# Moving one recurrent unit, keeping a second copy of q, and re-pacing the sample work in a hybrid decoder step

## The chip, the cores and the metric

The kernel runs on one core of a Trainium2 chip. The metric is the device time of one execution in microseconds (us). A core has five engines that each run their own instructions in order: PE (TensorE, the matrix multiplier, with its weight loads shown apart as PEld), DVE (VectorE), ACT (ScalarE), POOL (GpSimd) and SP (SyncE). SP does no arithmetic here: it issues most of the DMA transfers, in order, and a transfer that has to wait holds up those behind it. PE writes into PSUM banks, the other engines move results from there to SBUF, and DMA moves data between SBUF and DRAM.

## What is computed

One inference step of one decoder layer, for a prompt of 2048 tokens and for 8 sample requests of 4 tokens each, in float32:

```
a = rmsnorm(h); [qa|fa|ia|ga|qb|kb|vb] = a @ w_in          # 1024 -> 7 x 512
h = h + concat(HGRN2(qa,fa,ia,ga), DilatedAttn(qb,kb,vb)) @ w_o
h = h + ConvFFN(rmsnorm(h))                                # 1024 -> 2816 -> 1024
h = h + sigmoid(rmsnorm(h) @ w_ple_gate) * (p @ w_ple_proj)
y = rmsnorm(h)
```

HGRN2 is a gated linear recurrence over the tokens, with 4 heads of width 128 and a 128x128 state per head. It is evaluated in chunks; its output is normalised, multiplied by the gate made from `ga`, and put into `mix`. DilatedAttn is softmax attention with 8 heads of width 64 over three dilations (the last 128 tokens, every 4th of 512, every 16th of 2048). The sample requests do the same with a carried state and a window of cached keys and values.

## The kernel before

**Stages.** Three stages follow each other: the projections (`in_phase`, called once per block of tokens: block 0 is tokens 0 to 1023, block 1 the rest and the 32 sample tokens), attention (`attn_phase`), and the trunk (output projection, ConvFFN, embedding gate). A product of float32 matrices is made of three matmuls on parts that were split in two.

**Projections.** `ORDERS` gives the order of the seven groups of a block. The groups with two letters (`qa fa ga`) are made with features on the partitions, in 12 tiles of 24 matmuls each (`feature_group`); the others (`i q k v`) with tokens on the partitions, one tile per 128 tokens (`token_group`). After each tile the generator yields, and the main program runs one or two steps of the recurrence (`pace` says how many). In block 1 the accumulators rotate over two PSUM buffers. In this stage a scheduler sets the order of each engine's instructions, from priorities.

**Recurrent units.** `hgrn_unit(u, heads)` handles 512 tokens for two of the four heads. There are eight units (0 to 7), each of 11 steps: loads; three level steps of many small matmuls with DVE work on their results; two steps that finish the local matrix and transpose the keys; two that update the state and make the output; normalisation; and, in the last step, transposes and the product with the gate `g`. Units 0 to 3 are done before the marker `"H"` in `ORDERS[1]`, which stands after `ga`; units 4 to 6 beside `q k v`. Unit 7 is done in the attention stage, in a variant called `apart` (more and smaller steps, one rsqrt done on POOL, its matmuls on two PSUM banks called `s1` and `s2`).

**Attention.** Four pairs of heads (p = 0 to 3) are worked through in blocks (p, di, c) of four residues each: c is a chunk of 512 queries; for di = 0 the queries of a block are one residue mod 4 of the chunk (`qs[:, hh, 512*c + r : 512*c + 512 : 4]`, every fourth value in memory), for di = 1 they are 128 neighbours. A block has 4 units (8 where its keys are over 256 wide), 40 units per pair. One turn of the main loop starts one unit: its scores (two matmuls per head, with q as the weights and the high and low part of the keys moving), a masked row minimum on DVE, the exponential on ACT, transposes on PE two or three units later and the product with the values some units after that. `stage` loads q and k of a chunk from DRAM into two stage tiles, and `stack` splits them into `qS`, `kH`, `kL` (rounding and subtracting on POOL, casting keys on ACT). `merge` combines the two dilations. The PE order of this stage is written out by hand; the other engines' order is the scheduler's.

**Side work in attention.** `others()` gives steps that are put between the turns: 33 steps of unit 7, then 43 of `attn_sample` (the sample requests' attention, of which 32 each load up to 1 MB of cached keys or values into one of four `skt` tiles and multiply with them), then 17 of `hgrn_sample`. One step is done per turn in the first 29 turns and every second turn from there.

**Memory.** Six stage tiles rotate: two from each of two pools, and the two tiles `ssq` and `rb` of the projections. The pools of the attention stage take the memory that the projections leave; before the change unit 7's pools stay open beside them until unit 7 is done.

## Time and profile before

| what | us |
|---|---|
| median of 3 runs | 2956.08 |
| lowest and highest run | 2954.88, 2963.84 |
| the profiled execution | 2961.47 |
| its span, first to last instruction | 2959.4 |
| PE busy | 2887.6 (98% of the span) |
| DVE / ACT / POOL busy | 2154.3 / 1317.7 / 692.0 |
| stretches of the span: block 1's projections with recurrent units | about 375 to 806 |
| attention (pairs p = 0, 1, 2, 3 start at) | 806 (807.7, 899.4, 986.8, 1082.3) |
| trunk | about 1170 to 2959 |

The profile has a page with sums over the whole execution, and views that answer for a stretch of time: busy times by window, single instructions in order of time, the waits of an engine and what ended them. Busy time of one instruction reaches from its start to the end of its result, so two pipelined matmuls overlap: what a matmul costs the engine is read from the distance of two starts. `PEclk` is the share of the full TensorE clock that was granted in a stretch. DMA share is the mean busy share of 16 DMA engines; it can read a little over 1.

### The profile page before, as it was taken

Reading aid. Unit: us, or ns where it says so; the run is one execution under the profiler, and the core shown is the slowest. Engines: PE = TensorE matmul, PEld = TensorE weight load, DVE = VectorE, ACT = ScalarE, POOL = GpSimd, SP = SyncE. Lnnn points to the kernel's source line nnn. Section 1 sums busy time; section 2 is a strip of 40 time slices with the busy share of each in tenths; the row PEclk is TensorE's granted clock in tenths of the full one; section 3 lists DMA queues with packets and bytes.
Section 4 is the critical chain, followed back from the end, with each engine's and each line's share of the span. In section 5 each row is a group of like instructions: output and inputs, shape, how many; then the busy total and the mean of one; then the engine's idle time right before and its main releaser. Section 6 shows DMA issues by size and latency. Waiting matters only on the chain. (4 is left out here: it accounts for less than half of the span.)

```text
span 2959.4 us, 52469 instructions
## 1 busy us (share of the span) xinstructions
PE 2887.6 (98%) x18895; PEld 2697.3 (91%) x18895; DVE 2154.3 (73%) x4684; ACT 1317.7 (45%) x2856; POOL 692.0 (23%) x842
## 2 busy tenths in 40 slices
PE   8999999999989999999999999999999999999998
PEld 8987789987776678999999999999999999999998
DVE  6656857747685567579987889776679777778787
ACT  5333423222376676335444444544444544444453
POOL 1343322212343463003334332000102000101001
PEclk9999999999999999999999999999999999999999
DMA  5898633334549986775765668777779777778784
GB/s 182 296 355 302 220 105 104 109 92 130 173 123 272 253 208 200 263 260 190 243 200 192 207 216 292 238 237 239 257 241 313 245 235 244 260 246 297 262 283 148
DMA packets 341171, 660.92 MB, mean 223 GB/s; under 512 B 62960, under 2 KB 136816, under 8 KB 339120
## 3 DMA queue, kind: packets, MB, share of 16 engines
q1 hardware_dynamic: 297760, 452.13, 48.1%
q0 software_dynamic: 36944, 136.89, 14.3%
q10 hardware_dynamic: 6208, 68.56, 6.4%
q8 instruction: 149, 2.44, 0.3%
q14 instruction: 110, 0.90, 0.1%
HBM read 509.46 MB, written 213.92 MB: 244 GB/s over the span
## 5 line engine op out<-in xcount | busy, mean ns | idle before, releaser
L154 PE MATMUL mm<-w 128*128 128x348 f32 (+3 forms) x3620 | 1160.6, 321 | 0.8 <-DVE w L1493 0.7
L155 PE MATMUL mm<-w 128*128 128x348 f32 (+3 forms) x3492 | 1111.8, 321 | 1.7 <-DVE w L192 1.6
L153 PE MATMUL mm<-w 128*128 128x348 f32 (+3 forms) x3492 | 1103.0, 322 | 10.1 <-ACT s L1289 5.9
L154 PEld LDWEIGHTS mm<-w 128*128 128x128 f32 x3620 | 680.7, 188 | 3.2 <-DVE w L1493 1.4
L153 PEld LDWEIGHTS mm<-w 128*128 128x128 f32 x3492 | 653.0, 188 | 18.2 <-ACT s L1289 8.6
L155 PEld LDWEIGHTS mm<-w 128*128 128x128 f32 x3492 | 655.4, 188 | 3.3 <-DVE w L192 2.6
L192 DVE TENSOR_TENSOR w<-raw,w 128x512 fp32r<-128x512 f32 x586 | 425.0, 731 | 177.5 <-ACT w L191 166.1
L191 ACT CAST w<-raw 128x512 fp32r<-128x512 f32 x586 | 360.8, 621 | 418.2 <-PE mm L155 290.8
L1331 POOL DMA_DIRECT2D w<-wd_d x231 | 123.7, 536 | 897.4 <-PE mm L155 791.4
L1347 DVE TENSOR_TENSOR h<-h,mm 128x348 f32<-128x348 f32 (+1 forms) x504 | 247.5, 507 | 44.3 <-PE mm L155 42.8
L840 ACT ACTIVATE P<-P,st 128x256 f32<-128x256 f32 (+3 forms) x256 | 134.1, 527 | 68.0 <-DVE st L839 66.1
L839 DVE CUSTOM_DVE_ANT_0 P<-S,mask 128x256 f32<-128x256 f32 (+3 forms) x256 | 105.0, 448 | 72.8 <-PE S L835 45.3
L1289 ACT COPY s<-mm 128x348 f32<-128x348 f32 (+1 forms) x198 | 87.9, 444 | 156.3 <-PE mm L155 156.3
L358 PE MATMUL mm<-wl,xh 128*128 128x512 f32 x352 | 140.4, 400 | 0.1
L357 PE MATMUL mm<-wh,xh 128*128 128x512 f32 x352 | 140.2, 401 | 0.0
L359 PE MATMUL mm<-wh,xl 128*128 128x512 f32 x352 | 139.8, 398 | 0.0
L153 PE MATMUL mm<-xh,wh 128*128 128x384 f32 (+2 forms) x384 | 124.6, 329 | 6.8 <-ACT xh L253 5.0
L155 PE MATMUL mm<-xh,wl 128*128 128x384 f32 (+2 forms) x384 | 124.3, 327 | 3.5 <-DVE wl L278 3.4
L154 PE MATMUL mm<-xl,wh 128*128 128x384 f32 (+2 forms) x384 | 124.1, 326 | 0.1
L192 DVE TENSOR_TENSOR dw<-draw,dw 128x512 fp32r<-128x512 f32 x77 | 74.3, 967 | 55.8 <-ACT dw L191 55.4
L278 DVE TENSOR_TENSOR wl<-wraw,wh 128x512 fp32r<-128x512 f32 x104 | 86.6, 852 | 33.7 <-POOL wh L159 28.9
L159 POOL TENSOR_SCALAR wh<-wraw 128x512 fp32r<-128x512 f32 x96 | 76.6, 811 | 135.9 <-PE mm L154 47.9
(369 smaller groups left out, 5087.3 us busy)
## 6 DMA issues: line engine op xcount, KB each, us to landing
w<-wd_d POOLq DMA_DIRECT2D x231, 512.0 KB, 5.4
wd_d<-dw SPq DMA_DIRECT2D x77, 512.0 KB
out_sk_dram<-in_cache_k_dram ACTq DMA_DIRECT2D x56, 584.0 KB
out_sv_dram<-in_cache_v_dram ACTq DMA_DIRECT2D x56, 584.0 KB
raw<-in_w_gate_dram SPq DMA_DIRECT2D x110, 256.0 KB
raw<-in_w_up_dram SPq DMA_DIRECT2D x110, 256.0 KB
wraw<-in_w_in_dram SPq DMA_DIRECT2D x104, 256.0 KB
raw<-w_gate_d SPq DMA_DIRECT2D x88, 256.0 KB
```

The source lines that it names most:

```text
L153: PE.matmul(ps, lhsT=wh, rhs=xh, start=first, stop=False, skip_group_check=read)
L154: PE.matmul(ps, lhsT=wh, rhs=xl, start=False, stop=False, skip_group_check=read)
L155: return PE.matmul(ps, lhsT=wl, rhs=xh, start=False, stop=last, skip_group_check=read)
L191: A.copy(w[:, 0], raw)
L192: V.tensor_sub(w[:, 1], raw, f32(w[:, 0]))
L357: PE.matmul(ps, lhsT=xh[k][:, js], rhs=wh, start=k == 0, stop=False)
L358: PE.matmul(ps, lhsT=xh[k][:, js], rhs=wl, start=False, stop=False)
L359: ins = PE.matmul(ps, lhsT=xl[k][:, js], rhs=wh, start=False, stop=k == NK - 1)
L839: V.tensor_tensor_reduce(pe, s[:, w * i:w * i + w], bl.mask, 1.0, 3e38, ALU.add, ALU.min, mn)
L840: recent[:] = [A.activation(pe, pe, AF.Exp, bias=mn, scale=-1.0, accum_out=st[:, bl.r, hh, 0:1])]
L1331: G.dma_start(t, wd_d[p][n - 1])
L1347: V.tensor_add(o, o, acc[m][:, :H])
```

## The change

- The marker `"H"` moves ahead of `ga` in block 1, so units 0 to 3 run beside `i qa fa` (44 steps in 34 yields) and units 4 to 7 beside `ga q k v` (44 steps in 36 yields). Unit 7 is an ordinary unit now; `apart` is not used for a unit any more. A second marker `"A"` starts the first part of `attn_phase` where `"H"` did before.
- The gate `g` of a unit is loaded shortly before its last step, not at its beginning, since `ga` of block 1 is made after the unit has begun.
- The pools of the recurrence are closed before the pools of attention are opened.
- q is kept a second time for di = 0 of chunks 0 and 1, ordered by residue, so that the 128 queries of a residue lie side by side: `q0r` for the first chunk of pair 0 (made on POOL from `q0`), `res[0]` and `res[1]` for the others (`by_residue`, one ACT cast of 128 x 1024 each, seven in all). The scores of these blocks read their weights from there. For that, pool `a_f` has 4 buffers in place of 3, a pool `a_q` is added, and the tile `st` has 5 buffers in place of 6.
- The 60 steps of sample work that are left start at turn 7, in three of seven turns.
- In `attn_sample`, the eight copies that lay out q are issued within the first four key steps.

```diff
-ORDERS = ("qa fa ga v q k i".split(), "i qa fa ga H q k v".split())
+ORDERS = ("qa fa ga v q k i".split(), "i qa fa H ga A q k v".split())
...
+            if name == "A":
+                yield "attention"
+                continue
...
-            for nm, src in (("f", ha_d[1]), ("g", ha_d[2])):
-                t[nm] = ld.tile([128, 512], F32, name="h" + nm)
-                SP.dma_start(t[nm], src[:, h, u0:u0 + 512])
+            t["f"] = ld.tile([128, 512], F32, name="hf")
+            SP.dma_start(t["f"], ha_d[1][:, h, u0:u0 + 512])
...
-        for _ in range(3 if apart else 2):
-            yield
+        yield
+        for h in heads:
+            g = st[h]["g"] = ld.tile([128, 512], F32, name="hg")
+            SP.dma_start(g, ha_d[2][:, h, u0:u0 + 512])
+        yield
...
+        def by_residue(c):
+
+            A.copy(res[c].rearrange("p h (r i) -> p h r i", r=4),
+                   f32(qS[:, :, 512 * c:512 * c + 512]).rearrange("p h (i r) -> p h r i", r=4))
...
+        res = [pq.tile([128, 2, 512], F32R, name=f"qr{c}") for c in range(2)]
...
+            G.tensor_copy(q0r[:, hh].rearrange("p (r i) -> p r i", r=4), f32(q0[:, hh]).rearrange("p (i r) -> p r i", r=4))
...
-                    self.q = lambda hh: qs[:, hh, 512 * c + r:512 * c + 512:4]
+                    qr = q0r if head else res[c] if c < 2 else None
+                    self.q = lambda hh: (qr[:, hh, 128 * r:128 * r + 128] if qr else
+                                         qs[:, hh, 512 * c + r:512 * c + 512:4])
...
                     at(x, lambda p=p, c=c: stack(c, *staged.pop(0)))
+                    if c < 2:
+                        at(x + 4, lambda c=c: by_residue(c))
...
                     at(x - 4, lambda c=c: stack(c, *staged.pop(0), tc.keep_in_program_order))
+                    if c < 2:
+                        at(x - 2, lambda c=c: by_residue(c))
...
-    pace = itertools.chain([1] * 46, (33 * (i + 1) // 26 - 33 * i // 26 for i in range(99)))
+    pace = itertools.chain((44 * (i + 1) // 34 - 44 * i // 34 for i in range(34)), (44 * (i + 1) // 36 - 44 * i // 36 for i in range(99)))
...
-            side = hgrn(4, 7, *psum)
+            side = hgrn(4, 8, *psum)
+        elif x == "attention":
...
+    for h in range(4):
+        SP.dma_start(O["ps"][h], S[h])
+    hgrn_st.close()
     in_st.close()
...
-    rest += (pool("a_d", 2), pool("a_r", 1), pool("a_s", 3), pool("a_t", 8), pool("a_f", 3), pool("a_e", 2),
-             pool("a_w", 3),
+    rest += (pool("a_d", 2), pool("a_r", 1), pool("a_s", 3), pool("a_t", 8), pool("a_f", 4), pool("a_e", 2),
+             pool("a_w", 3), pool("a_q", 1),
...
-        yield from hgrn(7, 8, from_pool(pps, "s1", "s2"), from_pool(pps, "s1"), from_pool(pps, "s2"), apart=True)
...
-            if turn % 2 == 0 or turn < 30:
+            if turn > 6 and turn * 3 % 7 < 3:
                 first(side, 1)
```

How the change moves instructions is shown at three places. The numbers of the lines shift by up to 18 with the change.

The first is PE in block (p=0, di=0, c=1), the third block of attention, from the transposes (`PT`) ahead of it on. Before:

```order
L847 MATMUL PT<-c_ident,P 128x128 x6
L859 MATMUL acc<-pt,v 64x128 x4
L496 MATMUL s_8976<-hM,hF 64x3x32 x8
L834 MATMUL S<-kH,qS 128x256
L835 MATMUL S<-kL,qS 128x256
```

The same place with the change:

```order
L861 MATMUL PT<-c_ident,P 128x128 x6
L873 MATMUL acc<-pt,v 64x128 x4
L848 MATMUL S<-kH,qr_9022 128x256
L849 MATMUL S<-kL,qr_9022 128x256
...
L861 MATMUL PT<-c_ident,P 128x128 x8
L873 MATMUL acc<-pt,v 64x128 x4
L986 MATMUL s_9285<-skt,qb 32x512 x4
```

Unit 7's level matmuls (`hM,hF`) are gone from between the units, the scores take q from the copy by residue (`qr`), and the first sample step (`skt,qb`) stands in this block, where before it came in the last block of pair 0.

The second is the SP queue of transfers at the end of the projections: `stage` are the stage tiles of chunk 1 and 2 of pair 0, `ssq` and `rb` those of chunk 3, `ev` the results of the last token tiles, `v` the values, `skt` the sample requests' cached keys. Before:

```order
L705 DMA stage<-qT_d 64x2x512 x2
L392 DMA out_sv_dram<-v_s 4x512
L462 DMA hM<-ha_d 128x8x64
L392 DMA out_sv_dram<-v_s 4x512 x7
L397 DMA out_pv_dram<-ev 128x512
L398 DMA v_d<-ev 128x512
L705 DMA stage<-kT_d 64x2x512 x2
L705 DMA ssq<-qT_d 64x2x512 x2
L705 DMA rb<-kT_d 64x2x512 x2
```

With the change, later in the same token group:

```order
L984 DMA skt<-in_kT_w_dram 128x4x512 x4
L397 DMA out_pv_dram<-ev 128x512
L398 DMA v_d<-ev 128x512
...
L710 DMA stage<-qT_d 64x2x512 x2
L397 DMA out_pv_dram<-ev 128x512
L398 DMA v_d<-ev 128x512
L763 DMA v<-v_d 128x4x128
L766 DMA v<-v_d 32x4x128 x4
L710 DMA stage<-kT_d 64x2x512 x2
```

The first pair of `stage` rows is chunk 1's q and k in both orders. They stood five and six tiles of tokens ahead of the end of the projections and now stand around its last tile, behind four sample loads, and k behind the values too.

The third is ACT in the last blocks of pair 0, where chunks of pair 1 are stacked. Before:

```order
L840 ACTIVATE P,st<-P,st 128x256 x5
L719 CAST kH<-stage 128x4x128 x2
L849 COPY pt<-PT 128x512
L840 ACTIVATE P,st<-P,st 128x256 x2
L772 ACTIVATE w<-w 128x16
```

With the change:

```order
L724 CAST kH<-stage 128x4x128 x2
L1016 COPY sPTn<-s_9860 32x128
L854 ACTIVATE P,st<-P,st 128x256 x2
L729 CAST qr_9022<-qS 128x1024
L854 ACTIVATE P,st<-P,st 128x256
L784 ACTIVATE w<-w 128x16
```

A cast of 1024 values per partition (`qr`) now stands among the exponentials (`P,st`), and sample work (`sPTn`) stands there earlier than it did.

More of the change, by code (lines that the diff above doesn't have):

```diff
@@ L584, in hgrn_unit @@
         V.tensor_scalar(v, ssq, 1.0 / 128, EPS, op0=ALU.mult, op1=ALU.add)
-        r = (rsqrt_pow if apart else rsqrt_small)(sp, v.rearrange("p h c -> p (h c)"), [128, 8])
+        r = rsqrt_small(sp, v.rearrange("p h c -> p (h c)"), [128, 8])
         if apart:
@@ L724, in attn_phase @@
         yield
-        db, rp, sm, tp, fp, da, wk, pS, pA, pT = rest()
+        db, rp, sm, tp, fp, da, wk, pq, pS, pA, pT = rest()
         dp = itertools.cycle([lambda pool=pool: pool.tile([128, 2, 512], F32, name="stage") for pool in (da, da, db, db)]
@@ L732, in attn_phase @@
         q, k = first
-        q0, k0H, k0L = [fp.tile([128, 2, 512], F32R, name="cf") for _ in range(3)]
+        q0, k0H, k0L, q0r = [fp.tile([128, 2, 512], F32R, name="cf") for _ in range(4)]
         k0H, k0L = [t.rearrange("p h (r i) -> p h r i", r=4) for t in (k0H, k0L)]
+        res = [pq.tile([128, 2, 512], F32R, name=f"qr{c}") for c in range(2)]
         for hh in range(2):
@@ L922, in attn_phase @@
                 if bl.r == 0 and units[x].heads[0] == 0:
-                    both = sm.tile([128, 2, 4, 2, 2], F32, name="st", bufs=6)
+                    both = sm.tile([128, 2, 4, 2, 2], F32, name="st", bufs=5)
                 units[x].scores(both)
@@ L950, in attn_sample @@
         G.memset(qb, 0.0)
-        for p in range(4):
-            for hh in range(2):
-                rows = slice(64 * hh, 64 * hh + 64)
-                c = (2 * p + hh) * 4
-                V.tensor_copy(qb[rows, :, p, c:c + 4], qT_s[rows, p].rearrange("p (b t) -> p b t", t=4))
         mixs = cp.tile([128, 4, NS], F32, name="mixs")
@@ L965, in attn_sample @@
                     kt = kp.tile([128, 4, 512], F32, name="skt")[:, :, :widths[si]]
+                    for hh in range(2 if g + si == 0 else 0):
+                        rows = slice(64 * hh, 64 * hh + 64)
+                        c = (2 * p + hh) * 4
+                        tc.keep_in_program_order(
+                            V.tensor_copy(qb[rows, :, p, c:c + 4], qT_s[rows, p].rearrange("p (b t) -> p b t", t=4)))
                     SP.dma_start(kt, I[src][4 * g:4 * g + 4, :, p].rearrange("b d j -> d b j"))
@@ L1689, in others @@
     def others():
-        yield from hgrn(7, 8, from_pool(pps, "s1", "s2"), from_pool(pps, "s1"), from_pool(pps, "s2"), apart=True)
-        for h in range(4):
-            SP.dma_start(O["ps"][h], S[h])
-        hgrn_st.close()
         with ExitStack() as st:
```

## Prediction

> **What bounds the kernel now.** I read the page first, then busy times by window, then PE's waits, then single instructions in order of time.
>
> ```profile
> span 2959.4 us, 52469 instructions
> PE 2887.6 (98%) x18895; PEld 2697.3 (91%) x18895; DVE 2154.3 (73%) x4684; ACT 1317.7 (45%) x2856; POOL 692.0 (23%) x842
> ```
>
> PE is busy nearly throughout, so only work taken off PE, or one of its few gaps, can count. The windows show where the gaps are. Columns: stretch, its length, busy us of PE, PEld, DVE, ACT, POOL, granted clock, DMA share, GB/s. The first two are projections of block 1, the next two pair 0 of attention (cut where the third block starts), then pairs 1 and 2 in two halves each (di = 0, di = 1), then pair 3.
>
> ```profile
> 390.00:556.00 166.00, 165.01 (x1224) 153.46 (x1223) 117.29 (x362) 49.22 (x142) 42.84 (x56) 1.00 0.35 105
> 616.00:806.00 190.00, 189.96 (x1144) 147.94 (x1143) 113.28 (x349) 50.32 (x130) 42.59 (x56) 1.00 0.43 130
> 806.00:824.20 18.20, 15.81 (x109) 13.45 (x106) 13.72 (x61) 11.97 (x36) 14.06 (x14) 0.72 0.99 276
> 824.20:899.40 75.20, 68.56 (x585) 57.25 (x582) 61.74 (x183) 56.59 (x154) 37.82 (x40) 0.93 0.47 126
> 899.40:954.70 55.30, 49.61 (x424) 37.29 (x420) 27.95 (x95) 30.70 (x92) 9.37 (x13) 0.94 1.03 278
> 954.70:986.80 32.10, 32.10 (x319) 23.27 (x315) 22.24 (x85) 24.46 (x72) 29.60 (x35) 1.00 1.05 259
> 986.80:1050.40 63.60, 53.48 (x423) 39.41 (x422) 29.55 (x99) 32.33 (x94) 14.11 (x15) 0.89 1.00 258
> 1050.40:1082.30 31.90, 31.90 (x318) 22.48 (x314) 19.75 (x85) 26.92 (x75) 27.53 (x34) 1.00 0.88 189
> 1082.30:1170.00 87.70, 84.24 (x804) 72.15 (x801) 66.26 (x237) 56.53 (x180) 38.59 (x56) 0.98 0.66 180
> ```
>
> The projections have no gap worth naming. Attention takes 364 us, in which PE is idle 28.3 us (2.4, 6.6, 5.7, 10.1 and 3.5, length less PE busy), and the clock that was not granted is worth up to 22.5 us more (0.28 of 18.2, 0.07 of 75.2, and so on). In pairs 1 and 2 the DMA share is about 1. What PE waited for in attention:
>
> ```profile
> PE s L968 <- DMA skt<-in_kT_d_dram: 9.6, 6, 3.4
> PE S L834 <- DVE st L839: 6.0, 3, 4.2
> PE s L992 <- ACT sP L982: 3.6, 1, 3.6
> PE PT L847 <- ACT P L840: 3.5, 3, 2.0
> ```
>
> Sample loads are late by 9.6 us; the waits on DVE and ACT lie mostly in pair 0, where unit 7 shares those engines.
>
> **The move of unit 7.** Its matmuls in the projections, from the neighbouring units:
>
> ```profile
> 674.91 1.97 PE L496 MATMUL lv<-hM,hF 128*64 128x160 f32 x32
> 690.31 1.05 PE L496 MATMUL lv<-hM,hF 128*64 128x96 f32 x20
> 652.14 1.05 PE L564 MATMUL ms<-hv,kt 128*128 128x128 f32 x8
> 657.40 0.38 PE L576 MATMUL o<-S,hE 128*128 128x128 f32 x2
> 657.62 0.39 PE L575 MATMUL o<-hv,at 128*128 128x128 f32 x2
> 689.12 1.26 PE L598 MATMUL ms<-c_ident,at 128*128 128x128 f32 x8
> 698.44 0.68 PE L539 MATMUL lv<-hE,hF 128*64 128x64 f32 x8
> ```
>
> 96 level matmuls at 0.06 are 5.7; 16 state products 2.1; 16 pairs at 0.22 from start to start 3.5; 16 of L539 1.3; 8 transposes of L598 1.2, and 8 of L552 as many: 15, less some overlap at their ends, 14. PE is full there, so this is **+14 us** (12 to 15). DVE is the engine that could turn it into more: it is busy 117 of 166 us while three units pass; with four, a unit being at most a third of that and by its share of the second window's 113 nearer 30, it has some 147 in 180 us, 82%. An eviction that comes late behind level work stalls PE, since only two PSUM buffers rotate; at 71% the stalls were under 1 us (166.00 against 165.01). I add **+1** (0 to 8). Below nothing is excluded: no wait in the projections goes away.
>
> In attention unit 7 took about 17 us of PE, part of it at half clock:
>
> ```profile
> 815.89 2.51 PE L496 MATMUL s<-hM,hF 128*64 128x160 f32 x16
> 823.46 0.83 PE L496 MATMUL s<-hM,hF 128*64 128x96 f32 x16
> ```
>
> Two groups like the first (4.9 us) stand ahead of 824.2, the other 12 us behind it.
>
> **The first 18 us of attention.** Taking 4.9 us out of them gains nothing, I think, because the third block waits for keys of chunk 1. Before, their load was issued 33 us ahead; with the change it stands behind the last token tile's stores and the values:
>
> ```profile
> 772.69 1.24 SPq L705 DMA_DIRECT2D stage<-kT_d  x2
> 801.90 1.24 SPq L705 DMA_DIRECT2D stage<-qT_d  x2
> 811.43 2.37 SPq L754 DMA_DIRECT2D v<-v_d  x4
> 816.98 2.14 ACT L719 CAST kH<-stage 128x512 fp32r<-128x512 f32 x2
> 818.91 3.37 POOL L720 TENSOR_TENSOR kL<-stage,kH 128x512 fp32r<-128x512 f32 x2
> ```
>
> In the order of the change the load follows the values' rows, so issue is at about 813.8, the data some 4 us later, then cast 2.1 and subtraction 3.4: 823.5, against 822.3 before. Queued behind the k load are chunk 2's stage loads; behind the cast on ACT, exponentials. I take **+1** (-4 to +5). PE then idles some 8 us. The granted clock of 0.72 here shows that a thin start costs clock, and it will again.
>
> By the Trainium skill (TensorE: Matmul & The Clock Gate, section "HAM oscillation — how this bites in real kernels") an idle time of over about 3.4 us brings the half clock; this window's 0.72 agrees as far as it goes, and an estimate by that page is a further 1.7 us lost at the start (3.4 us at half).
>
> **q by residue.** Two score matmuls of 128 columns and two of 256, with q at every fourth value and with q side by side, read from start to start:
>
> ```profile
> 1082.86 0.40 PE L834 MATMUL S<-kH,qS 128*128 128x128 f32 x1
> 1083.09 0.40 PE L835 MATMUL S<-kL,qS 128*128 128x128 f32 x1
> ...
> 955.01 0.27 PE L834 MATMUL S<-kH,qS 128*128 128x128 f32 x1
> 955.12 0.27 PE L835 MATMUL S<-kL,qS 128*128 128x128 f32 x1
> ...
> 1002.07 0.40 PE L834 MATMUL S<-kH,qS 128*128 128x256 f32 x1
> 1002.30 0.39 PE L835 MATMUL S<-kL,qS 128*128 128x256 f32 x1
> ...
> 955.52 0.28 PE L834 MATMUL S<-kH,qS 128*128 128x256 f32 x1
> 955.64 0.28 PE L835 MATMUL S<-kL,qS 128*128 128x256 f32 x1
> ```
>
> 0.23 against 0.11, and 0.23 against 0.12. The change touches 8 blocks of 16 matmuls: 128 x 0.115 = 14.7 us less PE time, 3.7 in each pair. The first block of pair 0 (1.9) is lost in the wait above.
>
> The Trainium skill (SBUF — State Buffer, section "Door 1: The DMA port swizzle") says that four fp32 values may be strided over for free, and that each access on a new 16-byte line pays. The rows disagree with the first half: this stride is four values and doubles the distance. By that half the saving would be nothing and the sum 13 us worse.
>
> The price is on ACT: seven casts of 1024, two of this row's each, 2.3 us:
>
> ```profile
> L719 ACT CAST kH<-stage 128x512 fp32r<-128x512 f32 x20 | 21.9, 1141 | 5.1 <-DMA stage<-kT_d 3.8 <-PE S L834 1.3
> ```
>
> ACT is busy 24.46 of 32.10 us where they go, so 4.6 more per pair still fit. Exponentials queue behind a cast and PE's transposes wait for those; I take +1 per pair in pairs 1 and 2 (0 to 4.6). The two POOL copies for `q0r` follow the rounding of `q0`, over 40 us ahead of attention:
>
> ```profile
> L159 POOL TENSOR_SCALAR cf<-ssq x2: 610/611/612, 762.5 to 763.1; 128x512 fp32r<-128x512 f32 x2
> ```
>
> They, the `st` buffers, the later `g` loads and the moved `qb` copies I cost at nothing: each has a whole step or more of other work as cover (1 to 2 us each without).
>
> **Sample steps.** One that multiplies costs PE about 1.06:
>
> ```profile
> 1000.49 1.06 PE L968 MATMUL s<-skt,qb 128*32 128x512 f32 x8
> ```
>
> By the two orders, pair 0 gets some 11 more of them (+12), pair 1 two fewer (-2), pair 2 eight fewer and some small ones (-7), pair 3 one small step fewer (-1).
>
> **The sum for attention.** Pair 0 after 824.2: -12 (unit 7), -1.8 (q), +12 (steps), -6 of its 6.6 idle and 5.3 lost clock, since DVE and ACT have no unit 7: -8. Pair 1: -3.7, -2, +1, and -4 of 5.7 idle and 3.3 lost clock would be -9; but DMA is saturated there and two of 15 loads fewer, some 0.9 MB each at the window's 259 to 278 GB/s, give about 7 us: -6. Pair 2: -3.7, -7, +1, and -6 of 10.1 idle and 7.0 lost clock, half of what the missing loads could free: -15. Pair 3: -3.7, -1, -1: -6. With the +1 at the start: -34 (bounds -20, where nothing of idle time or clock comes back but pair 0's, to -55, where nearly all does). With +15: **-19 us**.
>
> The profiled execution took 2961.5 us by the table of times, 5.4 above the median of the runs. 2961.5 - 19 = 2942.5; less 5.4 is **2937**. A difference under 0.3% (9 us) cannot be told from none here.
>
> **Rivals.**
> 1. *The gaps nearly all close.* With the loads begun 60 us earlier and spread at 3/7, DMA and PE both run full; attention -55, less +14: 2956 - 41 = 2915. For it: DMA stood at 0.47 in pair 0's rest, so there is room. Against: in pairs 1 and 2 it was at 1.0 already.
> 2. *Nothing to see.* PE's order is fixed, and a shorter score only waits longer for masking and exponentials ahead of it, as the 6.0 and 3.5 us above show, or the 12.9 us of the scores in the sum are taken by q casts on ACT: -19 + 12.9 = -6, or 2950. For it: the rows of L834 and L847 among the waits. Against: in the di = 1 halves PE is busy throughout (32.10 of 32.10). The Trainium skill's free stride (SBUF — State Buffer) would give this number too, as scores that cost PE the same with either q; the rows above speak against it, and it has 0.02 of this rival's chance.
> 3. *Slower: sample loads block the SP queue.* An `skt` load waits for one of four buffers, and stage, value and coefficient loads wait behind it in the same queue. The order puts four of them ahead of chunk 1 at once, and the sample work begins while pair 0's chunks still come in. If each of the 32 loads makes PE wait 1.5 us, 48 us, the result is +29: 2985. It decides from 28 us of new waits on. Against: the worst such wait was 3.4 us and the sum 9.6, with the same queue and a higher rate. The change not doing what it says (q still strided) is excluded by its order.
>
> **How the numbers follow.** Forecast 0.62, rival 1 0.10, rival 2 0.19, rival 3 0.09. The range goes from rival 1's 2915, less a little, to rival 2's 2950 and 7 us of DVE stalls in the projections on top: 2913 to 2957. Faster 0.72 (forecast and rival 1), same 0.19, slower 0.09.
>
> **What would show it.** Right: projections end about 15 us later with PE still full; the scores of chunk 0 and 1 at 0.11 to 0.12 from start to start; a wait of PE of some 8 us ahead of the third block; pair 2 the largest gain; the `skt` wait under 9.6. Wrong: gaps of PE on evictions in the feature groups; waits of PE on stage or value loads; exponentials late behind `qr` casts; or no wait at the start, which would give 5 to 8 us more.

## The result and the profile after

| | us |
|---|---|
| before, median of 4 runs (lowest, highest) | 2957.8 (2954.9, 2963.8) |
| changed, median of 4 runs (lowest, highest) | 2989.9 (2988.6, 2991.6) |
| ratio, 95% interval | 1.0101 [1.0088, 1.0114] |
| span of the profiled execution, before and changed | 2959.4, 2986.8 |

The change makes the kernel slower by 32 us; the forecast was 19 us faster. Where the 27 us of span come from is read off the first score of attention (the start of its weight load) and the end of its last block: 807.7 and 1170.6 before, 830.2 and 1198.8 now. The projections take 22.5 us more (forecast 15), attention 5.7 us more (forecast 34 less), the trunk 1 us less. Over attention (807 to 1170 before, 830 to 1198 now) PE is busy 335.0 and 315.3 us and idle 28.0 and 52.7: its work fell by 20 us, as the shorter scores and unit 7's move were meant to bring about, and its idle time rose by 25.

Busy times by window of the changed kernel: the middle of block 1's projections, the start of attention up to the third block, the third block, and the third block of pair 1 and of pair 2 (chunk 2). Columns as in the prediction: stretch, length, PE, PEld, DVE, ACT, POOL, clock, DMA share, GB/s.

```profile
500.00:600.00 100.00, 94.74 (x733) 88.14 (x732) 78.74 (x243) 31.52 (x93) 24.40 (x33) 1.00 0.36 109
830.20:847.60 17.40, 10.95 (x56) 8.64 (x54) 6.88 (x37) 10.50 (x30) 6.41 (x7) 0.71 0.91 245
847.60:863.20 15.60, 10.86 (x68) 6.99 (x68) 8.02 (x24) 10.38 (x29) 13.68 (x13) 0.74 1.11 236
937.40:963.60 26.20, 16.28 (x130) 11.95 (x128) 9.06 (x26) 8.90 (x24) 2.48 (x2) 0.82 1.08 268
1030.80:1060.20 29.40, 18.61 (x132) 11.72 (x128) 8.99 (x24) 8.11 (x20) 7.51 (x6) 0.83 0.84 203
```

Before the change PE was full in the first of these stretches:

```profile
500.00:600.00 100.00, 100.00 (x768) 96.45 (x768) 76.56 (x239) 31.81 (x93) 24.42 (x31) 1.00 0.38 113
```

Now 5.3 of its 100 us are idle. The other four hold 32 us of PE idle time. What PE waited for in attention (us in total, times, longest):

```profile
PE s L1037 <- DVE som L1033: 9.9, 1, 9.9
PE PT L792 <- DVE pt L863: 9.9, 3, 9.2
PE S L848 <- DVE st L853: 6.3, 5, 2.6
PE PT L861 <- ACT pt L863: 5.9, 6, 1.6
PE PT L861 <- ACT P L854: 3.9, 4, 1.7
PE PT L861 <- DVE pt L863: 3.2, 3, 1.3
PE PT L861 <- ACT wt L794: 2.9, 3, 1.6
PE S L848 <- ACT kH L724: 2.9, 1, 2.9
PE s L986 <- DVE qb L983: 2.8, 1, 2.8
```

The waits for sample loads that led this list before (9.6 us) are gone. In their place PE waits for DVE: twice for 9 to 10 us, for two DVE results of unlike kinds. That suggests that DVE itself stood still. The single instructions around the first of these waits, by engine (start, duration, [idle before, what ended it]):

```profile
946.25 0.48 SPq L799 DMA_DIRECT2D cf<-coef_d  x1
949.35 0.47 SPq L799 DMA_DIRECT2D cf<-coef_d  x1
958.07 2.48 POOL L804 TENSOR_TENSOR o<-o,cf 128x512 f32<-128x512 f32 x2 [28.08 <-DMA cf<-coef_d]
960.58 0.69 DVE L806 TENSOR_TENSOR o<-o,o 128x512 f32<-128x512 f32 x1 [12.66 <-POOL o L804]
961.19 0.74 DVE L1033 SCALAR_TENSOR_TENSOR som<-s,sl,shm 128x512 f32<-128x512 f32 x1
961.99 1.89 PE L1037 MATMUL s<-ssel,som 128*128 128x16 f32 x8 [9.92 <-DVE som L1033]
```

The two loads of the merge's coefficients (256 KB each) are issued at 946.3 and 949.4; the second lands 8.7 us later, at 958.07. POOL multiplies for 2.5 us, and only then can DVE do the final add, L806. It had been at the head of DVE's queue for 12.7 us, and `som`, the score masks and the copies of `pt` stood behind it though their inputs were there. PE needs `som` and stands as well. No step of this chain is new. DVE stands in the same way ahead of the other long wait: L806 at 1039.4 follows 9.0 us of idle time that ended with POOL's multiply, and PE's 9.2 us wait ends at 1040.9.

The part of the prediction on the scores holds. Three scores of pair 2, chunk 0, a matmul of 128 columns each:

```profile
1016.67 0.28 PE L849 MATMUL S<-kL,qr 128*128 128x128 f32 x1
1016.78 0.27 PE L848 MATMUL S<-kH,qr 128*128 128x128 f32 x1
1016.89 0.28 PE L849 MATMUL S<-kL,qr 128*128 128x128 f32 x1
```

They are 0.11 us apart, as forecast; with q strided it was 0.23. And the start of attention:

```profile
815.55 3.36 SPq L984 DMA_DIRECT2D skt<-in_kT_w_dram  x4
826.68 1.81 SPq L710 DMA_DIRECT2D stage<-qT_d  x2
833.77 4.96 SPq L766 DMA_DIRECT2D v<-v_d  x4
841.50 1.24 SPq L710 DMA_DIRECT2D stage<-kT_d  x2
847.62 0.38 PE L848 MATMUL S<-kH,qr 128*128 128x256 f32 x1 [2.88 <-ACT kH L724]
```

Chunk 1's keys are asked for at 841.5, 11 us after the first score (before the change at 772.7, 35 us ahead of it), and the third block starts 17.4 us after the first (16.5 before).

### The profile page after: what moved, and what is told of

It reads as the page before. It is cut to its first block, busy times and chain, and to the rows that moved or that the text cites. A ratio compares the mean times of both kernels' runs of the same rounds, so it can differ in the third digit from the quotient of the medians.

```text
span 2986.8 us, 52532 instructions
## 1 busy us (share of the span) xinstructions
PE 2884.2 (97%) x18895; PEld 2684.5 (90%) x18895; DVE 2153.4 (72%) x4695; ACT 1332.8 (45%) x2863; POOL 696.3 (23%) x843
## 3 DMA queue, kind: packets, MB, share of 16 engines
q0 software_dynamic: 36944, 136.89, 14.1%
## 5 line engine op out<-in xcount | busy, mean ns | idle before, releaser
L359 PE MATMUL mm<-wh,xl 128*128 128x512 f32 x352 | 139.7, 397 | 0.0
L861 PE MATMUL PT<-c_ident,P 128*128 128x128 f32 x568 | 86.4, 290 | 16.7 <-ACT pt L863 5.9
```

What stands on the lines that cost most here:

```text
L359: ins = PE.matmul(ps, lhsT=xl[k][:, js], rhs=wh, start=False, stop=k == NK - 1)
```

## The experiments

Eighteen kernels were run. Each is the changed kernel with the edit that is named, unless it says otherwise. The theories, with the letters that the expectations use (E and F came up with the runs that test them):

- A: DVE stands at the merge's add, and the shorter scores only bring PE to that wait sooner.
- B: the second layout of q costs as much as it brings.
- C: the second layout works as forecast, and something else costs 30 us.
- D: the coefficients are late because the DMA engines are full; A is only the place where it shows.
- E: more unit steps beside qa and fa fill DVE, and the projections' evictions come late.
- F: chunk 1's keys come late because of where their tiles lie in memory.

The table has the ratio of each to the kernel before, and from the trace the start of attention and its length, split into the residue blocks of chunks 0 and 1 (touched by the second q), those of chunks 2 and 3, and the window blocks (di = 1). A block's time is that from its first score to the next block's.

| run | ratio [95% interval] | attention starts | length | c0, c1 | c2, c3 | window |
|---|---|---|---|---|---|---|
| before | 1 | 807.7 | 362.9 | 79.9 | 144.5 | 138.6 |
| changed | 1.0101 [1.0088, 1.0114] | 830.2 | 368.6 | 68.9 | 153.6 | 146.2 |
| e1 strided q | 1.0072 [1.0055, 1.0089] | 825.0 | 366.0 | 79.9 | 147.3 | 138.9 |
| e2 add on POOL | 1.0028 [1.0016, 1.0039] | 830.9 | 347.7 | 75.4 | 126.9 | 145.5 |
| e3 coefficients by POOL's queue | 1.0078 [1.0060, 1.0095] | 829.2 | 359.6 | 75.6 | 137.0 | 147.2 |
| e4 steps late | 1.0070 [1.0054, 1.0087] | 829.1 | 358.8 | 68.4 | 139.7 | 150.8 |
| f1 e2 + e4 | 1.0036 [1.0023, 1.0050] | 826.0 | 346.1 | 72.4 | 123.8 | 149.8 |
| f2 e2 + e1 | 1.0033 [1.0021, 1.0045] | 825.4 | 347.3 | 89.5 | 121.2 | 136.8 |
| f3 before + add on POOL | 1.0009 [0.9997, 1.0022] | 804.5 | 364.7 | 79.0 | 140.0 | 145.4 |
| f4 e2 + units thinner | 1.0028 [1.0017, 1.0039] | 822.5 | 346.2 | 73.9 | 126.6 | 145.9 |
| g1 e2 + casts on DVE | 1.0057 [1.0038, 1.0075] | 828.9 | 351.5 | 86.4 | 126.3 | 138.9 |
| g2 before + unit 7 beside | 1.0050 [1.0033, 1.0068] | 841.3 | 341.8 | 72.4 | 139.1 | 130.3 |
| g3 quarter of the loads | 1.0008 [0.9991, 1.0025] | 824.1 | 340.7 | 69.7 | 126.5 | 144.4 |
| g4 f4 + e1 + e4 | 1.0027 [1.0015, 1.0040] | 825.5 | 347.8 | 80.1 | 123.6 | 144.2 |
| h1 e2 + three cf | 1.0024 [1.0014, 1.0034] | 825.7 | 344.5 | 75.1 | 127.5 | 142.0 |
| h2 g4 + three cf | 1.0014 [1.0002, 1.0026] | 826.0 | 347.0 | 75.4 | 127.5 | 144.5 |
| h3 h2, early steps | 1.0017 [1.0005, 1.0028] | 823.1 | 346.3 | 86.3 | 125.3 | 134.8 |
| h4 h2 with casts | 1.0022 [1.0010, 1.0033] | 822.9 | 350.4 | 67.6 | 129.8 | 152.9 |
| j1 h3 + qb first | 1.0008 [0.9998, 1.0018] | 827.8 | 342.8 | 81.2 | 128.0 | 133.9 |
| j2 h2 + qb first | 1.0000 [0.9989, 1.0011] | 822.9 | 341.9 | 77.6 | 125.2 | 139.1 |

The start of attention scatters: kernels with the same projections (changed, e2, e3, e4, f1, g1, g3) have it at 824.1 to 830.9, most of it from before 360 us. So single traces tell projections apart to some 5 us only; the waits inside them are the safer reading. The mean of these seven starts, 828.3, lies 22.2 us behind the mean of the two kernels with the projections of before (before and f3, 806.1), so that the 22.5 us are not scatter. Differences in us below are between medians that were measured at different times, and the kernel before moved from 2956.3 to 2960.2 between them; where a few us matter, the ratios decide.

### e1 to e4: what of the change costs attention its gain

```diff
 e1, in by_residue:        - A.copy(res[c]..., f32(qS...))      + pass    (and no q0r; self.q always strided)
 e2, in merge:             - (G if p == 3 else V).tensor_add    + G.tensor_add
 e3, in merge:             - SP.dma_start(cf[...])              + G.dma_start(cf[...])
 e4, main loop:            - turn > 6 and turn * 3 % 7 < 3      + turn > 30 and turn % 2 == 0
```

> The changed kernel without the second layout of q: no cast into qr0/qr1 on ScalarE, no copy into q0r on GpSimd; every score of a residue block reads q with a stride of four again. Theory A (the 15 us that the score matmuls give up are lost because PE arrives earlier at a wait that other engines set, the merge's final add on DVE): time within 5 us of the changed kernel's 2990, the first residue blocks of each pair back at 0.23 us per matmul and the PE waits behind the add shorter by about as much. Theory B (the casts on ScalarE cost more than they bring): faster by 5 to 15 us. Theory C (the second layout works as forecast, and something else costs 30 us): slower by 9 to 14 us, some 3002.

2981.0 us, 9 us faster than with the second layout. Attention is 2.6 us shorter, the rest lies in where attention starts and is within the scatter. The touched blocks are back at 79.9, 11 us more; the window blocks give back 7.3, chunks 2 and 3 6.3. C falls, since undoing the second layout makes the kernel faster, not slower. Between A and B f2 decides.

> The changed kernel with the merge's final add on GpSimd for all four pairs, so that nothing on DVE waits for the coefficient loads. Theory A (DVE stands at this add, in its in-order queue, and PE behind DVE): faster by 15 to 25 us, to about 2970, the waits of PE on som and pt of 9 to 10 us gone. Theory D (the loads themselves are late because the DMA engines are full, and some other step takes the wait): faster by 0 to 8 us, the same gaps of PE under another releaser.

2969.4 us, 20.5 us faster: A holds. The start of attention is the same, its length falls by 20.9. The 9 us waits are gone; PE's longest waits are now the following, and no instruction of DVE waits for L804 any more:

```profile
PE PT L861 <- ACT P L854: 8.3, 6, 3.3
PE PT L861 <- ACT pt L863: 5.1, 4, 1.8
PE PT L792 <- DVE pt L863: 3.4, 1, 3.4
```

> The changed kernel with the coefficient loads issued by GpSimd instead of SyncE, past the queue of sample, stage and value loads. If the loads are late because they stand behind others in SyncE's queue: the merge's multiply waits 3 us or less in place of 28 and 13, and the kernel is faster by 10 to 20 us. If they are late because the 16 DMA engines are full (share 1.08 between 937 and 964 us): the wait shrinks by half at most and the time changes by under 6 us.

2984.3 us, 5.5 us faster (attention 9 us shorter): by the time the second answer. But the queue has a part: past it, what DVE waits for POOL at the add falls in all from 45.8 to 23.8 us. The longest of these waits is still 9.5 us (12.7), and PE still stands 6.8 us at `som`. The Trainium skill (DMA: Bandwidth & Descriptors, section "Issuing engines are not separate DMA queues") says that transfers of all issuing engines run on the same 16 DMA engines, so that another issuer saves only the issue time; the small gain agrees with it, the halved waits of DVE go beyond it.

> The changed kernel with sample steps as dense and as late as before the change (from turn 31 on, every second turn) in place of three of seven from turn 7. If the early start costs (4 MB of sample loads ahead of chunk 1's keys, 11 us of PE idle in the first 33 us of attention): the third block starts within 10 us of the first in place of 17.4, pair 0 takes about 75 us in place of 93, and the kernel is faster by 5 to 12 us, less what pairs 1 to 3 lose by denser loads. If only the mean load of the DMA engines counts: the same within 5 us, or slower, since 25 steps' loads move into a shorter stretch.

2982.0 us, 8 us faster, but not by the first reading: the third block still starts 17.7 us after the first (846.8 against 829.1). The run cannot say whether sample loads delay chunk 1, since the first four of them (4 MB, one for each `skt` tile) are issued at 814.5 here too; the later start only moves the others. Most of the gain is in chunks 2 and 3, where the coefficient chain is.

### f1 to f4: do the parts add up

```diff
 f1 = e2 + e4      f2 = e2 + e1      f3 = the kernel before + e2
 f4 = e2 and, for the pace beside i, qa and fa (33 steps of in_phase):
- (44 * (i + 1) // 34 - 44 * i // 34 for i in range(34))
+ (22 * (i + 1) // 9 - 22 * i // 9 for i in range(9)), (22 * (i + 1) // 24 - 22 * i // 24 for i in range(24))
```

> The changed kernel with the merge's add on GpSimd and the sample steps from turn 31 on, every second turn: the two edits that were each faster (by 20.5 and 8 us). If they cure different waits (the late start the 10 us of idle time before chunk 1's blocks, the add those in pairs 1 and 2) the sum holds: some 2961. If the late start mostly relieved the same coefficient loads, no gain beyond the add's: 2966 to 2972.

2967.5 us, ratio 1.0036 against 1.0028 with the add alone: no further gain. So the late start had mostly relieved the same chain.

> The changed kernel with the merge's add on GpSimd, and q strided again (no second layout). Theory A says that the shorter scores were lost because PE came earlier to the same wait on DVE; with that wait gone they must show: without the second layout slower by 8 to 14 us than with it, 2978 to 2983. Theory B (ScalarE's casts and GpSimd's copies cost as much as they bring, whatever the add does): the same as with it or faster, 2958 to 2971.

2968.4 us, the same as with the second layout: B, and A's part on the scores falls. The trace shows the exchange: without the casts the touched blocks take 14.1 us more, the window blocks 8.7 less, chunks 2 and 3 5.7 less. Pair 1's window blocks, first with the casts (e2), then without (f2):

```profile
966.90:1003.50 36.60, 31.02 (x333) 23.26 (x331) 22.54 (x92) 29.29 (x75) 31.30 (x38) 1.00 1.01 267
```

```profile
960.10:991.00 30.90, 30.01 (x331) 23.26 (x330) 22.18 (x92) 25.31 (x73) 27.55 (x35) 1.00 0.96 271
```

With the casts for the next pair in them PE is idle 5.6 of 36.6 us, without 0.9 of 30.9. ACT is busy 4 us more, which is the two casts. The effect is not the same everywhere: by the starts of the blocks, pair 0's window blocks take 4.2 us more with the casts and pair 1's 5.6, pair 2's, with two casts as well, only 0.2.

> The kernel before with the merge's add on GpSimd. If DVE stood at this add there too (its trace shows DVE waiting 17.9 us for GpSimd's multiply in the merge), faster by 3 to 10 us. If only the changed kernel's earlier PE made it a wait that counts: within 3 us of the kernel before.

2961.0 us, ratio 1.0009, an interval that holds 1: no gain. DVE's wait for the merge was there before the change too, 17.9 us where it is 45.8 with the change:

```profile
L794 DVE TENSOR_TENSOR o<-o,o 128x512 f32<-128x512 f32 x12 | 9.7, 811 | 17.9 <-POOL o L792 17.9
```

The longest of these waits was 7.2 us before the change, and PE had no wait over 4.2 us in attention. That PE did not need DVE in that time is the reading of this; the run shows that the wait cost nothing.

> The changed kernel with the merge's add on GpSimd, and units 0 to 3 no longer spread evenly over the steps of i, qa and fa (44 steps of theirs in 33): 22 beside the nine steps of i, 22 beside the 24 of qa and fa. Theory E (DVE is full while the feature groups of qa and fa are evicted, 20.0 of 20 us at 560, and PE waits 5 us there): projections end 5 to 10 us earlier, 2960 to 2965. If the units' own matmuls are longer whatever stands beside them, the same as with the add alone, 2967 to 2972; if i has no room for them, later.

2963.0 us; the ratio, 1.0028, is that of e2, so the time does not tell them apart. The trace does. PE's waits in the projections of block 1, with even pace (e2) and with the thinner one (f4):

```profile
PE mm L153 <- DVE ev L313: 3.0, 2, 1.9
PE lv L498 <- POOL hM L488: 1.1, 1, 1.1
```

```profile
PE lv L498 <- DVE blk L515: 0.7, 1, 0.7
PE mm L155 <- DVE wl L278: 0.7, 2, 0.4
```

The wait for the feature groups' evictions (L313) is gone, and PE's idle time from 410 us on falls from 5.9 to 2.1 us. E holds, for about 4 of the 22.5 us.

### g1 to g4: the cause behind the add, the casts, and unit 7 alone

```diff
 g1 = e2 and, in by_residue:  - A.copy(res[c]...)          + V.tensor_copy(res[c]...)
 g2 = the kernel before and:  - side = hgrn(4, 7, *psum)   + side = hgrn(4, 8, *psum)     (44 steps beside q, k, v)
                              - yield from hgrn(7, 8, ..., apart=True)
                              - turn % 2 == 0 or turn < 30 + turn > 30 and turn % 2 == 0
 g3, in attn_sample:          - SP.dma_start(kt, I[src][4 * g:4 * g + 4, ...])
                              + SP.dma_start(kt[:, :1], I[src][4 * g:4 * g + 1, ...])     (and rhs=kt[:, 0]; values alike)
 g4 = f4 + e1 + e4
```

> The changed kernel with the merge's add on GpSimd, and the seven casts into qr0 and qr1 on DVE in place of ScalarE. With strided q the residue blocks of chunks 0 and 1 took 14 us more and the window blocks 9 us less than with the casts. If the window blocks are late because the casts (7 x 2.06 us) stand ahead of exponentials and copies on ScalarE: they fall from 145.5 to about 138 us, and the kernel is faster by 5 to 8 us than with the add alone. If window blocks are limited by DVE's masking as much (ScalarE waited 64 us for it): no gain, 0 to 4 us slower.

2973.2 us, ratio 1.0057 against 1.0028. The window blocks fall to 138.9 as the first reading had it: the casts on ScalarE are what makes them late. But the gain turns up nowhere: the touched blocks rise from 75.4 to 86.4 us. The casts themselves are shorter there, 1.14 us (median) against 2.07 on ScalarE, so their own length is not what the touched blocks lose; what it is was not looked into. So the second layout pays on neither engine. GpSimd was not tried.

> The kernel before with one part of the change alone: the eighth unit beside the projections (units 4 to 7 in 44 steps beside q, k and v), nothing of it in attention, where the sample steps begin at turn 31. By the prediction's terms: projections end 14 to 15 us later, attention about 12 us shorter, the kernel 0 to 5 us slower than before. If a unit beside the projections costs what the changed kernel's trace shows (projections from 359.9 to 830.2 against 359.0 to 805.4, 24 us longer): 8 to 14 us slower than before.

2971.7 us, 14 us slower than before, in another way than either reading. The last projection matmul starts only 6.3 us later than before (811.7 against 805.4), but the eighth unit is not done by then, and its rest runs alone:

```profile
819.77 1.55 PE L496 MATMUL lv<-hM,hF 128*64 128x96 f32 x16 [6.20 <-POOL hM L486]
839.45 1.97 PE L598 MATMUL ms<-c_ident,at 128*128 128x128 f32 x8 [5.13 <-DVE at L590]
```

Attention starts at 841.3, 33.6 us later, and takes 21.1 us less. Pair 0 is 68.6 us instead of 91.7: without unit 7 it is 23 us shorter, where its matmuls are 17. So the beginning of attention has more to give than the prediction's -12, if its data are there in time, as they were here.

> The changed kernel, add on DVE as it is, with a quarter of each sample load: one of the four sequences' keys or values is loaded and multiplied four times (the output of the decode rows is not the reference's). If full DMA engines are why the coefficients come late (share 1.08): GpSimd's multiply waits under 3 us in place of 28 and 13, and the kernel is faster by 15 to 30 us. If the coefficient chain is late by its own steps (transposition, store, load: five stages on four engines) and not by the load of the DMA engines: under 8 us.

2960.6 us, 29 us faster, with the add still on DVE: the load of the DMA engines by sample data is behind most of the loss, as D has it. (The kernel leaves out three quarters of the sample requests' keys and values.) POOL's wait for coefficients and DVE's for POOL, over the whole of attention, first of the changed kernel, then with a quarter of the loads:

```profile
  DMA cf<-coef_d: 110.0, 14
  DVE o L806: 45.8, 11
```

```profile
  DMA cf<-coef_d: 80.4, 15
  DVE o L806: 23.3, 11
931.00:957.50 26.50, 25.00 (x202) 17.85 (x201) 15.72 (x41) 12.92 (x33) 7.46 (x6) 1.00 0.40 123
```

DVE's waits halve, the longest falls from 12.7 to 3.6 us, and no wait of PE over 2.6 us is left. POOL still waits long for coefficients, up to 11 us at a time and not under 3 as expected, but little stands behind it. Since e3 halves DVE's waits in all as well and gains 5.5 us, either the few long waits count and not their sum, or the smaller loads relieve more than the coefficients; no run separates the two. The last row is the counterpart of 937.40:963.60 above: DMA share 0.40 in place of 1.08, PE idle 1.5 in place of 9.9, the full clock in place of 0.82. The start of attention is hardly better: chunk 1's keys are asked for at 834.1, 10.0 us after the first score, and the third block starts 15.9 us after the first, though 1 MB of sample loads stands ahead in place of 4.

> The changed kernel with all that has been faster or no slower so far: add on GpSimd, sample steps from turn 31 on every second turn, units 0 to 3 thinner beside qa and fa, q strided. If the parts add up as their traces say (projections 3 us shorter than the changed kernel's, attention 343 to 347 us): 2955 to 2962, no better than the kernel before; if starting late and strided q still give something on top of the add: 2948 to 2955.

2964.9 us, ratio 1.0027: the parts do not add up to more than the add alone. Pair 0 takes 82.9 us where g2's takes 68.6.

### h1 to h4: why attention starts slowly

`a_f` (three `cf` tiles before, four with `q0r`) lies in memory ahead of `a_e`, the first pair of rotating stage tiles. A fourth tile moves `a_e` up by 4 KB less the `st` tile that is gone. Byte addresses in each partition, from the built programs:

| | first stage tile | second stage tile |
|---|---|---|
| before | 110080 | 114176 |
| changed | 114048 | 118144 |
| three `cf` | 109952 | 114048 |

The projections' rope buffers (`sg`, `ra`, `rb`, `oT`) end at 119072, where the weights `wh` begin. The rope is done with the group k. Changed, the second tile reaches over two of the weight buffers, which v's matmuls read to the end.

```diff
 h1 = e2 and:  - q0, k0H, k0L, q0r = [fp.tile(...) for _ in range(4)]   + q0, k0H, k0L = [... range(3)]
               - pool("a_f", 4)                                        + pool("a_f", 3)
 h2 = g4 with the same three buffers      h3 = h2 without e4      h4 = h2 with the casts
```

> The changed kernel with the merge's add on GpSimd, without q0r and its fourth cf buffer (chunk 0 of pair 0 reads q strided, as before the change). The buffers of cf lie ahead of those of stage; with three instead of four, chunk 1's stage tiles lie on the buffers of the rope (sg, oT, free when the last rope of k is done) and not on two of the nine weight buffers of the projections (wh, free when the last projection is done). Theory F (chunk 1's keys come late for this reason): the stage load of chunk 1's keys is issued before 800 us in place of 841, the third block of attention starts 13 us after the first in place of 17.7, and the kernel is faster by 4 to 8 us than with the add alone. If the 4 MB of sample loads ahead of it are the cause: the load is issued in time but lands late, and under 2 us are gained.

2966.0 us, ratio 1.0024 against 1.0028. F holds for chunk 1 and brings little:

```profile
780.32 1.29 SPq L710 DMA_DIRECT2D stage<-qT_d  x2
781.71 1.22 SPq L710 DMA_DIRECT2D stage<-kT_d  x2
...
836.94 1.23 SPq L710 DMA_DIRECT2D stage<-kT_d  x2
```

Chunk 1's keys are asked for at 781.7 in place of 842.6 (e2), ahead of the sample loads (811.1), and the third block starts 14.6 us after the first. e1 has four buffers but not the copies into `q0r`, and asks for these keys late too, at 836.1; g3 has a quarter of the sample loads, and asks at 834.1. So the late request comes from the place in memory, not from the copies or the sample loads. One thing stays open: q's load is late as well in the kernels with four buffers (826.7 in the changed one), though its tile lies on the rope's buffers alone. But chunk 2's load is the next in line, and PE meets another wait in the third block:

```profile
PE s L985 <- DVE qb L982: 4.7, 1, 4.7
```

These copies, two ahead of each of the first four sample steps and pinned to their place, stand on DVE behind the masks of the scores next to them, though what they read was there long before.

> Add on GpSimd, units 0 to 3 thinner beside qa and fa, sample steps from turn 31 on, q strided, three cf buffers. By theory F pair 0 falls from the 82.9 us of the same kernel with four buffers to about 70 us (68.6 in the kernel before with the eighth unit beside the projections), and the kernel from 2965 to 2950 to 2955, faster than before by up to 7 us. If the four buffers cost nothing: 2962 to 2967.

2963.7 us, ratio 1.0014; pair 0 84.9 and not 70. The third block now takes 7.8 us, but the fourth 20.2, since POOL's low half of chunk 2's keys is 4.4 us late; and later in pair 0, where the sample steps begin, PE waits 5.6 us for `qb`.

> The same with the sample steps as the change has them, three turns of seven from turn 7. Late or early steps made no difference with the add on GpSimd (2967.5 to 2969 us). If chunk 1's keys are in time by theory F, the early sample loads collide only with chunks 2 and 3: 2950 to 2958, pairs 1 to 3 shorter by 5 us than with late steps and pair 0 longer by as much. If the early loads delay chunks 1 to 3: 5 to 10 us slower than with late steps.

2964.7 us, ratio 1.0017: early or late makes no difference here either; PE waits 6.8 us for `qb`.

> The same as the second, late steps, but with the casts into qr0 and qr1 on ScalarE (and q strided only for chunk 0 of pair 0). With and without the second layout of q there was no difference (2969 and 2968 us): residue blocks 14 us shorter, window blocks and those of chunks 2 and 3 as much longer. Theory B, that this exchange is fixed: within 4 us of the strided kernel. If the gain was only masked by the late start of pair 0: 5 to 10 us faster than it.

2966.8 us: with the casts again no gain (touched blocks 7.8 us less, window blocks 8.4 more). B a third time.

### j1 and j2: the copies into qb

```diff
 j1 = h3, j2 = h2, each with the eight copies back behind G.memset(qb, 0.0), as before the change
```

> The kernel with the add on GpSimd, units 0 to 3 thinner beside qa and fa, q strided, three cf buffers and early sample steps (ratio 1.0017 to the kernel before), with one more part of the change undone: the eight copies into qb stand together at the start of the sample phase, as before the change, and no longer two beside each of the first four loads in program order. PE waited 6.8 us for them in pair 0. If these copies are late only because DVE reaches them behind the masking of later scores: that wait is gone, pair 0 falls from 86.8 to 80 to 83 us, and the kernel comes to 2956 to 2961, no different from the kernel before (ratio 0.999 to 1.001). If chunk 2's stage loads are the next in line at the same place (issued at 822 and 837 us in the run with three buffers): under 2 us.

2960.9 us, ratio 1.0008 [0.9998, 1.0018]: the wait is gone, pair 0 is 83.8 us, 3 less.

> The same with sample steps from turn 31 on, every second turn (5.6 us of waits for qb in the run with three buffers, 4.8 for the low half of the keys). By the first reading 2956 to 2962 and pair 0 at 78 to 82 us; if the waits for keys take over, 2961 to 2966.

2956.3 us, ratio 1.0000 [0.9989, 1.0011]; pair 0 falls from 84.9 to 76.7. This is the best version, and it is no faster than the kernel before. None of the eighteen was faster than the kernel before. What PE waits for now:

```profile
PE s L1024 <- DMA skt<-in_v_d_dram: 6.3, 3, 3.3
PE S L847 <- POOL kL L725: 4.7, 2, 4.2
PE s L984 <- DMA skt<-in_kT_d_dram: 3.4, 3, 2.2
```

Of the change it keeps the eighth unit beside the projections, with the units thinner beside qa and fa; the second q, the early steps, the fourth buffer and the moved copies are undone, and the add is on POOL. Its attention is 21.0 us shorter than before (341.9 against 362.9), its start 15.2 us later; by these two sums it would be 6 us faster. Its profiled span is 2.2 us shorter than before (2957.2), the trunk having taken 3.6 more, and the runs show no difference.

## Why the prediction was wrong

| step | forecast | measured |
|---|---|---|
| projections (unit 7 +14, DVE +1) | +15 (12 to 23) | +22.5 |
| first three blocks | +1 | +0.9 |
| pair 0 with them | -7 | +1.3 |
| pair 1 | -6 | +5.4 |
| pair 2 | -15 | +1.5 |
| pair 3 | -6 | -2.5 |
| attention | -34 (-20 to -55) | +5.7 |

**Unit 7, +14: mis-sized.** By a sum over the trace from each start to the next, from 410 us to the last projection matmul, the units' matmuls take 80.0 us before and 98.4 changed. A seventh unit beside the six there would be 13.3 by count, which the prediction's 14 meets. Of the other 5, 1 is a group of transposes that stood behind the last projection matmul before; some 4 are matmuls that each take longer, the level matmuls 0.060 in place of 0.057 us, the transposes of L598 (now L603) 0.119 in place of 0.112 us, those of L552 0.113 in place of 0.095. Why they do was not tried. PE's idle time rises from 1.0 to 5.9 us.

**DVE, +1 (0 to 8): inside its range, for another reason than the one given.** The wait came where the prediction put it, on evictions, but not by a fourth unit beside q, k and v. It came beside qa and fa, where the change puts units 0 to 3 into 33 steps instead of 45; that part was read past in costing the move by one unit. f4 takes it away.

**First blocks, +1: right**, with 6.5 us of PE idle time where some 8 were forecast and a clock of 0.71. So was the late load of chunk 1's keys, but its cause was only half seen: the prediction had it wait behind stores and values in SyncE's queue; h1 shows that its tile lies on weights that the projections hold.

**q by residue, -14.7 and +2 for the casts: the scores right, the price wrong.** The matmuls come at 0.11, and the touched blocks shrink by 11 to 14 us (e1, f2). The step that failed is "4.6 more per pair still fit" on ACT. The casts took 2.08 us each (costed at 2.3), but ScalarE's free time was not where they stood: they made the window blocks 7 to 9 us longer, which goes when they leave ScalarE (g1). The way there, exponentials and PE's transposes queued behind a cast, is the prediction's own, priced at +2 in place of 7 to 9. The rest goes in chunks 2 and 3. The second rival had this exchange, without the loss that the other steps bring.

**Idle time that comes back, -6, -4 and -6: the step that decides.** The prediction took the sample loads that pairs 1 and 2 lose as a gain of DMA time, at the waits that the profile before showed, PE on `skt`. Those waits did go. It did not follow what else waits at a DMA share of 0.8 to 1.1: the coefficients, for which POOL's multiply stood idle for long before the change as well (126.7 us in all, 110.0 with it). With less work on PE the same lateness reached PE, through an add that blocks DVE: 21 us by e2, 29 with the loads themselves quartered (g3). The two gains overlap and do not add. The third rival named coefficient loads and 2985 us, but as a blocked SyncE queue in which `skt` loads wait for buffers; past that queue (e3) 5.5 us come back, against 20.5 by the add and 29 by the loads. That its number lies within 5 us of the measured 2990 is mostly luck.

**Costed at nothing.** The moved `qb` copies cost 2.8 us of waits in the changed kernel and 3 to 8 us of pair 0 where the start is otherwise in time (j1, j2). The reason given, "each has a whole step or more of other work as cover", overlooked that a copy pinned to its place waits for what stands ahead of it. `q0r` cost the 4 KB that moved the stage tiles.

**What stays open**: what lengthens the units' matmuls in the projections, which engine takes the rest of the scores' gain in chunks 2 and 3, and how much of g3's 29 us goes through the coefficients.

The Trainium skill's clock rule that the prediction cites (TensorE: Matmul & The Clock Gate, section "HAM oscillation — how this bites in real kernels") agrees where gaps are long: 0.82 and 0.83 in the two windows with waits of 9 to 10 us, 1.00 in g3's counterpart.

## What to carry to other kernels

When work is taken off the engine that is full, list what stands behind each in-order queue at a late input, not only what that engine waits for now: an add that waits for a load costs nothing until someone needs the instruction behind it, and moving that one add to the engine that feeds it was worth more here than any other single edit that keeps all of the work. A cheaper instruction pays only in the block that is bound by its engine; sum the blocks on both sides of the edit before booking it. A buffer added to a pool moves every pool behind it, and a tile that then lies on memory held longer makes its load late: compare addresses and last readers.

## What the runs showed of the hardware

Reading 128 weights at every fourth fp32 value takes a matmul of 128 columns from 0.11 to 0.23 us, in both directions of the edit, and a 128x1024 copy on ScalarE into the other order takes 2.08 us (1.14 on VectorE in g1, median). With the DMA share at 1.08, a 256 KB load issued at 949.35 us had not landed until 958.07; SyncE had issued another 1 MB sample load 2.6 us ahead of it.
